# Splitting two inner products of a Strassen-Winograd kernel a third time, in its first four stages

## The chip, the cores and the metric

The kernel runs on one core of a Trainium2 chip. The core has TensorE (PE; PEld is its weight load), VectorE (DVE), ScalarE (ACT), GpSimd (POOL) and SyncE (SP), each with its own instruction queue in order, and 16 DMA engines. On-chip data lies in SBUF; PE writes its products into PSUM, eight banks of 512 fp32 columns by 128 partitions. The metric is the device time of one execution in microseconds (us), the median of several runs.

## The reference

`x` has 16 x 512 = 8192 rows of 512, `router_logits` 8 values for each row, `expert_weights` eight matrices of 512 x 2048. The output is the sum of all experts' products, weighted by the softmax:

```python
probs = np.exp(router_logits - logits_max)
probs = probs / np.sum(probs, axis=-1, keepdims=True)
for e in range(n_experts):
    output += probs[:, :, e:e+1] * np.matmul(x, expert_weights[e])
```

With the weighted copies of `x` side by side this is one product of 8192 x 4096 by 4096 x 2048.

## The kernel before

**Two levels of Strassen-Winograd.** The large product is cut in halves in each of its three dimensions and made from seven products, named P1 to P7 (`product(r, q)`, r from 1 to 7), instead of eight. Rows come in 16 pairs of blocks of 256 (`HQ`), so each P has 16 instances, q from 0 to 15. An instance is again cut in two by two by two and made from seven *inner* products: 128 rows (`HP`) by 1024 contracted values (eight chunks of 128) by 512 columns, that is eight matmuls of 512 columns (`Product.step`). `STEPS` gives their order, 1, 5, 6, 2, 7, 3, 4. In Winograd's form some products are sums of earlier ones: 6, 7 and 4 are added by PE onto the bank that inner product 1 wrote ("x"), 3 onto that of 5 ("q"), 2 onto a copy ("b") of 1. Between these additions ACT or DVE takes the intermediate values out (`Product.post`, `post_alone` for P1).

**Operands.** The left operand of an instance (`Left`) is made by DVE from transposed rows `xT` and broadcast probabilities `pT`: two halves (`make`, tiles `z`, 2048 columns each), their difference `s2` (tile `d`) and `i` (a `z`). The right operand (`Right`) is a set of fp16 weight tiles `w`, some read, some summed by DVE (`inner_sums`). In an early part the instances P1 of q = 0 and 1 are computed in another way (loop over `n` and `e`, lines 308 to 331), in which the weights are read, transposes are made on PE, and ACT finally copies four banks out (line 331).

**Stages.** From then on the work runs in stages of mostly two instances, step by step in turn (`run`): 14 steps of eight matmuls. Stages 0 to 3 hold the P1 instances of q = 2 to 9, two in each; stage 4 pairs a P2 with a P1.

**Order of the work.** Each engine's queue keeps the program's order. DVE's background work (left operands, weight sums) stands in one queue of tasks with costs written into the code. `slack` advances a PE clock by 1.73 us (`SLOT`) for every step and takes tasks off the queue while DVE's clock is behind; `need` takes off everything up to an operand that a step is about to use; `evacuated` books an evacuation on DVE. Loads, stores and weight casts hang on a stage's step number: loads for the stage after next start after step 1 (`start_loads`), stores after 5, transposing DMAs after 7 (`finish_loads`), others through `hooks`, set by `at(stage, slot, ...)`.

**Buffers.** Weight tiles `w` 15 (`wpool`), `z` 8, `d` 3, `x` 10, `h` 12 (`hpool`: halves of results waiting for their store, and small temporaries), PSUM banks 8 (`bank`).

Of the kernel before, what the change touches and what calls it, by code (L numbers as in the profile page):

```python
# [31 lines left out]
def kernel(  # L32
# [7 lines left out]
    nc = tc.nc  # L40
    P = 128
    f16 = mybir.dt.float16
    f32 = mybir.dt.float32
    ADD, SUB, MUL = mybir.AluOpType.add, mybir.AluOpType.subtract, mybir.AluOpType.mult
# [5 lines left out]
    C = H // P  # L50
# [4 lines left out]
    HQ = 256  # L55
# [15 lines left out]
    K8 = 2 * C  # L71
    BLOCKS = ((0, 0), (1, 0), (0, 1), (1, 1))

    def h_tile(shape, dtype):
        return hpool.tile(shape, dtype, name="h", tag="h")

    def half():
        return h_tile([P, NB], f32)
# [16 lines left out]
    def note(i):  # L95
        last[i.ins.engine] = i.ins
        if ordered[0]:
            tc.keep_in_program_order(i)

    def dve(i):  # L100
        last[i.ins.engine] = i.ins
        tc.keep_in_program_order(i)

    act = dve

    def tt(o, a, b, op):
        dve(nc.vector.tensor_tensor(out=o, in0=a, in1=b, op=op))  # L107
# [15 lines left out]
    def bank():  # L123
        return psum.tile([P, NB], f32, name="ps", tag="ps")

    def mm(ps, z, w, start, stop):
        note(nc.tensor.matmul(ps, z, w, start=start, stop=stop, skip_group_check=True))  # L127
# [3 lines left out]
    def new_w():  # L131
        return wpool.tile([P, K8, NB], f16, name="w", tag="w")
# [31 lines left out]
    def inner_sums(b, t7=None):  # L164

        w = {1: b[0, 0], 2: b[1, 0], 3: b[1, 1], 7: t7 or b[0, 1]}

        def step(p, x, y):
            if p not in w:
                w[p] = new_w()  # L170
            tt(w[p], x, y, SUB)
        return w, {5: lambda: step(5, b[0, 1], b[0, 0]), 6: lambda: step(6, b[1, 1], w[5]),
                   4: lambda: step(4, b[1, 0], w[6]), 7: lambda: step(7, b[1, 1], b[0, 1])}

    def softmax(lg, J, pf):
        mx = h_tile([P, J], f32)
        dve(nc.vector.tensor_reduce(out=mx, in_=lg, axis=AX, op=mybir.AluOpType.max))
        tt(lg, lg, mx.unsqueeze(2).to_broadcast([P, J, E]), SUB)
        nc.scalar.activation(out=lg, in_=lg, func=mybir.ActivationFunctionType.Exp)
        sm = h_tile([P, J], f32)  # L180
        dve(nc.vector.tensor_reduce(out=sm, in_=lg, axis=AX, op=ADD))
        dve(nc.vector.reciprocal(out=sm, in_=sm))
        n = pf.shape[1]
        tt(pf, lg.rearrange("p j e -> p e j")[:, 0:n], sm.unsqueeze(1).to_broadcast([P, n, J]), MUL)
        return pf
# [35 lines left out]
    def early_p(t):  # L221
        if t == 0:
            return softmax(lg0[t], 4, cpool.tile([P, HE, 4], f16, name="ph0"))
        pf = softmax(lg0[t], 4, cpool.tile([P, HE, 4], f32, name="pf0"))
        odd = pf.rearrange("p e (q j) -> p e q j", j=2)[:, :, :, 1]
        tt(odd[:, 0:2], odd[:, 0:2], odd[:, 2:4], ADD)
        ph = cpool.tile([P, HE, 4], f16, name="ph1")
        dve(nc.vector.tensor_copy(ph, pf))
        return ph
# [16 lines left out]
    def diag_e(e):  # L246
        return diag(ph0[0][:, e].unsqueeze(2))

    def early_z0(e, d):
        for j in range(4):  # L250
            ps = bank()
            for c in range(C):
                mm(ps[:, ds(c * P, P)], xs0[:, j, ds(c * P, P)], d[:, j], c == 0, c == C - 1)
            evacuate(z0[j][:, e], ps.rearrange("p (c t) -> p c t", c=C), j)
# [5 lines left out]
    def diag_j(j):  # L260
        return diag(ph0[1][:, :, ds(j % 4, 1)])
# [46 lines left out]
    for n in range(2):  # L308
        ps = [bank() for _ in range(4)]
        for e in range(HE):  # L310
            if n == 0 and e < 2:
                early_z0(e + 2, ds_[e + 2])
                if e == 0:
                    ds_.append(diag_e(3))
            if n == 0 and e == 2:
                ph0.append(early_p(1))
                ds_ = [diag_j(j) for j in range(4, 8)]
                softmax_of_all()
                w, sums = inner_sums(b11, new_w())
            for c in range(C):  # L320
                for j in range(4):
                    mm(ps[j], z0[j][:, e, c], b11[e // 2, n][:, e % 2 * C + c, :],
                       e + c == 0, e == HE - 1 and c == C - 1)
            if n == 1:
                for j in ((4, 5), (6, 7), (), ())[e]:
                    early_xp1(j, ds_[j - 4])
                if e == 1:
                    sums[5]()
        for j in range(4):
            o = half()  # L330
            act(nc.scalar.copy(o, ps[j]))
            sp(kept[j // 2][n].rearrange("(p j) m -> j p m", j=2)[j % 2], o)

    ordered[0] = True
    SLOT = 1.73
    STEPS = (1, 5, 6, 2, 7, 3, 4)
    HP = HQ // 2
    LAG = 0.3
    queue = deque()
    clock = {"pe": 0.0, "dve": 0.0}  # L340

    class Task:


        def __init__(self, cost, make):
            self.cost, self.make, self.done = cost, make, False
# [10 lines left out]
    def need(task):  # L357
        if task is not None and not task.done:
            flush(task)
            clock["pe"] = max(clock["pe"], clock["dve"])  # L360

    def later(cost, make, first=False):
        t = Task(cost, make)
        (queue.appendleft if first else queue.append)(t)
        return t

    def slack():
        clock["dve"] = max(clock["dve"], clock["pe"])
        clock["pe"] += SLOT
        while queue and clock["dve"] < clock["pe"] - LAG:  # L370
            queue.popleft().run()

    def evacuated():
        clock["dve"] = max(clock["dve"], clock["pe"]) + 0.69


    x_dram = {}
# [48 lines left out]
    class Left:  # L426
# [6 lines left out]
        def make(self, k):  # L433
            if self.of is not None:
                need(self.of.task[k])
            t = self.t[k] = new_z()
            times(t, k, self.xb, self.pb)
            if self.less is not None:
                u = new_u()
                times(u, k, *self.less)  # L440
                tt(t, t, u, SUB)
            if self.of is not None:
                tt(t, self.of.t[k], t, SUB)
# [19 lines left out]
        def op(self, p):  # L463
            need(self.task[{1: 0, 5: 0, 6: "s2", 2: 1, 4: 1, 3: "i", 7: "i"}[p]])
            if p == 6:
                return self.s2
            t, i = {1: (self.t[0], 0), 5: (self.t[0], 1), 2: (self.t[1], 0), 4: (self.t[1], 1),
                    3: (self.i, 0), 7: (self.i, 1)}[p]
            return t[:, :, ds(i * HP, HP)]

    class Right:

# [100 lines left out]
    stages = []  # L573
    hooks, late = {}, {}
# [11 lines left out]
    lefts, xs, ps_, bases = {}, {}, {}, {}  # L586
# [69 lines left out]
    def start_loads(stage):  # L656
        if stage < len(stages):
            for p in stages[stage]:
                for load in p.loads:
                    load.begin()  # L660
# [13 lines left out]
    def queue_left(left):  # L674
        if not left.task:
            left.queue_make(0)
            left.queue_s2()
            left.queue_make(1)

    def queue_lefts(stage):  # L680
        if stage < len(stages):
            for p in stages[stage]:
                queue_left(p.left)

    def run(stage):
        some = stages[stage]
        for p in some:
            p.left.queue_i()
        n = 0
        for i in range(len(STEPS)):  # L690
            for p in some:
                for make in hooks.get((stage, n), ()):
                    make()
                p.step(p.steps[i])
                slack()
                p.post(p.steps[i])
                n += 1
                if n == 1:
                    queue_lefts(stage + 1)
                if n == late.get(stage, 1):  # L700
                    start_loads(stage + 2)
                if n == 5:
                    store_loads(stage + 1)
                if n == 7:
                    finish_loads(stage + 2)
# [12 lines left out]
    for i in range(0, 10, 2):  # L718
        k = add(product(2, rest[i]), product(2, rest[i + 1]))
# [9 lines left out]
    some = product(6, 15)  # L729
# [4 lines left out]
    some = product(4, 15)  # L734
# [16 lines left out]
    for q in range(16):  # L751
        k = k5 + 1 + q
# [223 lines left out]
    cols = [ds(i * NB // 2, NB // 2) for i in range(2)]  # L976
# [26 lines left out]
            post(p)  # L1003
    finish.step, finish.post = step_at_end, post_at_end

    need_first = [right[1].task[p] for p in (6, 7, 4)]
    for p in (2, 3):
        lefts[1, p].queue_make(0)
    queue.append(need_first[0])
    for p in (2, 3):  # L1010
        lefts[1, p].queue_s2()
    for p in (2, 3):
        lefts[1, p].queue_make(1)
    queue.extend(need_first[1:])
    start_loads(1)
    store_loads(0)
# [1 line left out]
    for k in range(len(stages)):  # L1018
        run(k)
# [28 lines left out]
```

## Time and profile before

| what | value |
|---|---|
| median of 3 runs | 1376.44 us (1376.37 to 1376.78) |
| profiled execution | 1376.57 us, span 1374.8 us |
| TensorE clock granted | 1.00 |
| PE busy / DVE / ACT / POOL | 1368.2 / 1109.0 / 183.1 / 411.9 us |
| matmuls `ps<-w,z` of 512 columns | 5400, mean 379 ns |
| stages 0 to 3, in the span | 40.26 to 136.9 us |

Rows of the profile name a line of the kernel, the engine, the operation, output tile and inputs, shapes, and the count; after the bar stand busy time, the mean duration of one in ns and the idle time of that engine just before, with what ended it. Line 127 is the helper that issues every matmul, line 107 the one that issues every `tensor_tensor` on DVE. A timeline row gives start, duration, engine, line and what ended the wait before it. Matmuls are pipelined: one of 512 columns is listed with 379 ns, but the next starts earlier than that. The time of a profiled execution holds some microseconds outside the span of its instructions.

### The profile page before, as it was taken

What the parts mean: (1) busy time and instruction counts of PE and PEld (TensorE: products, weight loads), DVE (VectorE), ACT (ScalarE), POOL (GpSimd) and SP (SyncE); (2) the same over time, 40 slices, a digit from 0 to 9 for tenths busy, and PEclk for the clock granted to TensorE, in tenths of its full rate; (3) what the DMA queues carried; (4) which work ended last, traced back from release to release, by engine and by line L of the source; (5) the groups of instructions that cost most, each with busy time, mean ns of one, the idle gap of its engine ahead of it and who ended that gap; (6) DMA issues with size and microseconds to landing.
All of it is one profiled execution on the core that took longest, in us unless ns stands there. A gap on an engine that the chain in (4) does not pass through costs nothing.

```text
span 1374.8 us, 17481 instructions
## 1 busy us (share of the span) xinstructions
PE 1368.2 (100%) x6390; PEld 622.4 (45%) x6390; DVE 1109.0 (81%) x1290; ACT 183.1 (13%) x317; POOL 411.9 (30%) x652
## 2 busy tenths in 40 slices
PE   9999999999999999999999999999999999999998
PEld 4444444444444444444444444444444444444444
DVE  5846757679889888888887988889889898988782
ACT  3221111100011111111111100000000000212221
POOL 3222333231223342434332122333333322232322
PEclk9999999999999999999999999999999999999999
DMA  9998999999898998998897997988898979998785
GB/s 181 218 259 215 213 252 261 252 294 379 239 313 254 266 315 250 278 263 238 255 274 263 333 395 214 232 239 209 227 233 227 241 211 312 249 187 179 167 148 101
DMA packets 191271, 338.02 MB, mean 246 GB/s; under 512 B 52944, under 2 KB 86992, under 8 KB 187472
## 3 DMA queue, kind: packets, MB, share of 16 engines
q0 software_dynamic: 88688, 185.12, 56.2%
q1 hardware_dynamic: 98464, 123.34, 30.7%
q10 hardware_dynamic: 4032, 28.44, 5.3%
q8 instruction: 50, 0.82, 0.3%
q14 instruction: 37, 0.30, 0.1%
HBM read 207.65 MB, written 156.43 MB: 265 GB/s over the span
## 4 chain that ended last, share of the span: by engine, by line
PE 98%; DMA 1%; DVE 0%; issue 0%; POOL 0%; ACT 0%; POOLq 0%
PE ps L127 98%; DMA w<-wd 1%; DMA w<-in_x_dram 0%; DVE h L107 0%; DVE z L241 0%; POOL w L121 0%; ACT h L1000 0%; DVE lg L281 0%; POOLq L1032 0%
## 5 line engine op out<-in xcount | busy, mean ns | idle before, releaser
L127 PE MATMUL ps<-w,z 128*128 128x512 f16 x5416 | 1177.2, 379 | 0.9 <-DVE h L107 0.8
L127 PEld LDWEIGHTS <-z 128*128 128x128 f16 x5416 | 529.8, 98 | 638.1 <-issue 1.1
L121 POOL DMA_DIRECT2D out_dram<-h x380 | 248.9, 672 | 753.4 <-ACT h L540 379.7
L107 DVE TENSOR_TENSOR h<-ps,h 128x512 f32<-128x512 f32 x415 | 282.5, 688 | 209.5 <-PE ps L127 194.5
L107 DVE TENSOR_TENSOR z<-xT,pT 128x2048 f16<-128x2048 f16 x220 | 266.9, 1217 | 12.7 <-DMA xT<-xs 10.1
L127 PE MATMUL ps<-w,d 128*128 128x512 f16 x880 | 199.1, 379 | 0.0
L127 PEld LDWEIGHTS <-d 128*128 128x128 f16 x880 | 86.1, 98 | 103.8
L107 DVE TENSOR_TENSOR z<-z,d 128x2048 f16<-128x2048 f16 x110 | 132.1, 1216 | 0.0
L107 DVE TENSOR_TENSOR w<-w 128x1024 f16<-128x1024 f16 (+2 forms) x92 | 100.8, 1102 | 3.2 <-DMA wd<-w 1.4
L527 ACT COPY h<-ps 128x512 f32<-128x512 f32 x90 | 52.8, 587 | 373.9 <-PE ps L127 326.6
L540 ACT COPY h<-ps 128x512 f32<-128x512 f32 x64 | 37.5, 587 | 485.8 <-PE ps L127 458.5
L107 DVE TENSOR_TENSOR z<-z,u 128x2048 f16<-128x2048 f16 x64 | 78.4, 1225 | 2.2
L107 DVE TENSOR_TENSOR d<-z 128x1024 f16<-128x1024 f16 x110 | 75.2, 685 | 5.9 <-PE ps L127 4.0
L107 DVE TENSOR_TENSOR u<-xT,pT 128x2048 f16<-128x2048 f16 x64 | 77.9, 1218 | 0.0
L523 ACT COPY h<-ps 128x512 f32<-128x512 f32 x90 | 52.8, 587 | 173.9 <-PE ps L127 171.1
L121 POOL DMA_DIRECT2D wd<-w x86 | 48.3, 585 | 33.1 <-DVE w L107 24.4
L121 POOL DMA_DIRECT2D w<-in_expert_weights_dram x65 | 48.9, 784 | 27.8 <-DMA wd<-w 18.0
L107 DVE TENSOR_TENSOR ps<-ps,h 128x512 f32<-128x512 f32 (+1 forms) x66 | 45.4, 689 | 13.0 <-PE ps L127 12.9
L121 POOL DMA_DIRECT2D kept<-h x56 | 30.8, 551 | 76.9 <-ACT h L527 46.9
L107 DVE TENSOR_TENSOR h<-h 128x512 f32<-128x512 f32 (+2 forms) x69 | 45.1, 675 | 0.2
L519 ACT COPY ps<-ps 128x512 f32<-128x512 f32 x45 | 25.6, 570 | 114.6 <-PE ps L127 114.6
L107 DVE TENSOR_TENSOR z<-z 128x2048 f16<-128x2048 f16 x32 | 39.2, 1225 | 1.1
(47 smaller groups left out, 98.4 us busy)
## 6 DMA issues: line engine op xcount, KB each, us to landing
out_dram<-h POOLq DMA_DIRECT2D x380, 256.0 KB, 6.2
pT<-p_dram SPq DMA_DIRECT2D x140, 256.0 KB, 6.1
w<-wd ACTq DMA_DIRECT2D x27, 1024.0 KB, 9.6
h<-kept SPq DMA_DIRECT2D x100, 256.0 KB, 5.4
xT<-x SPq DMA_DIRECT2D x87, 256.0 KB, 5.6
wd<-w POOLq DMA_DIRECT2D x72, 256.0 KB, 5.4
w<-in_expert_weights_dram POOLq DMA_DIRECT2D x35, 512.0 KB, 10.0
h<-out_dram SPq DMA_DIRECT2D x68, 256.0 KB, 5.5
```

What stands on the lines that cost most here:

```text
L107: dve(nc.vector.tensor_tensor(out=o, in0=a, in1=b, op=op))
L121: note(nc.gpsimd.dma_start(out=o, in_=i, **how))
L127: note(nc.tensor.matmul(ps, z, w, start=start, stop=stop, skip_group_check=True))
L519: act(nc.scalar.copy(self.banks["b"], x))
L523: act(nc.scalar.copy(o[tn], q if p == 5 else x))
L527: act(nc.scalar.copy(o[TN[p]], b if p == 2 else x))
L540: act(nc.scalar.copy(o[tn], b))
```

## The change

In stages 0 to 3, the inner products 1 and 5 of the two instances are no longer two products each. For each of the two, the pair of instances is taken as one product of 256 rows (128 of each instance) by 1024 by 512, which is cut a third time: rows between the two instances, the contracted values into two groups of four chunks, the columns into two halves of 256. Seven products of four matmuls of 256 columns take the place of two of eight matmuls of 512. Steps of the new level are called r1 to r7 here, in the order of `STEPS`, and inner products 1 and 5 take turns at each.

The new right operands are made once (`third_sums`, four `tensor_tensor` for inner product 1 and four for 5, each set in one further weight tile) in the early part, and `sums[5]` moves one `e` forward. The new left operands of a stage are four sums of 128 x 1024 (`Thirds.make`, one task of cost 2.76 for both inner products, since they lie in the two row halves of the same tiles). Each of the two inner products has a spare bank beside its two result banks: r1, r6, r7, r4 use the left 256 columns of it, r5 and r3 the right, and ACT or DVE moves the values on. DVE's queue is ordered anew, and the hooks of a stage's first four steps run at the small steps 0, 4, 7 and 11.

```diff
+    def third_sums(w):
+        t = new_w().rearrange("p (s c) (h n) -> p s c h n", s=2, h=2)
+        t = {5: t[:, 0, :, 0], 6: t[:, 0, :, 1], 7: t[:, 1, :, 0], 4: t[:, 1, :, 1]}
+        b = w.rearrange("p (k c) (h n) -> p k c h n", k=2, h=2)
+        tt(t[5], b[:, 0, :, 1], b[:, 0, :, 0], SUB)
+        tt(t[6], b[:, 1, :, 1], t[5], SUB)
+        tt(t[7], b[:, 1, :, 1], b[:, 0, :, 1], SUB)
+        tt(t[4], b[:, 1, :, 0], t[6], SUB)
+        return {**t, 1: b[:, 0, :, 0], 2: b[:, 1, :, 0], 3: b[:, 1, :, 1]}
...
                 w, sums = inner_sums(b11, new_w())
+                third = {1: third_sums(w[1])}
...
-                if e == 1:
+                if e == 0:
                     sums[5]()
+                elif e == 1:
+                    third[5] = third_sums(w[5])
...
-    def slack():
+    def slack(slot=SLOT):
         clock["dve"] = max(clock["dve"], clock["pe"])
-        clock["pe"] += SLOT
+        clock["pe"] += slot
...
+    class Thirds:
...
+        def make(self):
+            e0, e1 = ds(0, C), ds(C, C)
+            a, b = self.a.t[0], self.b.t[0]
+            for p, x, y, op in ((5, b[:, e0], b[:, e1], ADD), (6, None, a[:, e0], SUB),
+                                (3, a[:, e1], None, SUB), (7, a[:, e0], b[:, e0], SUB)):
+                o = self.s[p] = h_tile([P, C, HQ], f16)
+                x = self.s[5] if x is None else x
+                y = self.s[6] if y is None else y
+                tt(o, x, y, op)
+
+        def queue(self):
+            self.a.queue_make(0)
+            self.b.queue_make(0)
+            self.task = later(2.76, self.make)
+            for left in (self.a, self.b):
+                left.queue_s2()
+            for left in (self.a, self.b):
+                left.queue_make(1)
+
+        def op(self, p, part):
+            need(self.task)
+            a, b = self.a.t[0], self.b.t[0]
+            z = {1: a[:, 0:C], 2: a[:, C:K8], 4: b[:, C:K8]}.get(p)
+            return (self.s[p] if z is None else z)[:, :, ds(part * HP, HP)]
...
+    def by_thirds(stage):
+        some = stages[stage]
+        left = thirds[stage]
+        cols = [ds(i * HQ, HQ) for i in range(2)]
+        goals, spare, kept_ = {}, {}, {}
+        for i, (p, b) in enumerate(((1, "x"), (5, "q"))):
+            for product in some:
+                product.banks[b] = bank()
+            goals[p] = [product.banks[b] for product in some]
+            spare[p], kept_[p] = bank(), half()
+        slot = 0
+        for n, (r, p) in enumerate((r, p) for r in STEPS for p in (1, 5)):
+            if n in (0, 4, 7, 11):
+                for make in hooks.get((stage, slot), ()):
+                    make()
+                slot += 1
+                if slot == 2:
+                    queue_lefts(stage + 1)
+                    start_loads(stage + 2)
+            (g, h), t, keep = goals[p], spare[p], kept_[p]
+            x, q = t[:, cols[0]], t[:, cols[1]]
+            o = {1: x, 6: x, 7: x, 4: x, 5: q, 3: q, 2: g[:, cols[0]]}[r]
+            z, w = left.op(r, p // 5), third[p][r]
+            for c in range(C):
+                mm(o, z[:, c, :], w[:, c, :], r == 1 and c == 0, c == C - 1)
+            slack(0.4375)
+            if r == 1:
+                act(nc.scalar.copy(g[:, cols[0]], x))
+            elif r == 5:
+                act(nc.scalar.copy(keep[:, cols[1]], q))
+            elif r == 6:
+                act(nc.scalar.copy(keep[:, cols[0]], x))
+            elif r == 7:
+                evacuated(0.42)
+                tt(h[:, cols[1]], x, keep[:, cols[1]], ADD)
+            elif r == 3:
+                evacuated(0.42)
+                tt(g[:, cols[1]], q, keep[:, cols[0]], ADD)
+                if p == 1:
+                    some[0].post(1)
+            elif r == 4:
+                act(nc.scalar.copy(h[:, cols[0]], x))
+        some[1].post(1)
+        for product in some:
+            product.post(5)
+        return 4
...
     def queue_lefts(stage):
-        if stage < len(stages):
+        if stage in thirds:
+            if thirds[stage].task is None:
+                thirds[stage].queue()
+        elif stage < len(stages):
...
-        n = 0
-        for i in range(len(STEPS)):
+        n = by_thirds(stage) if stage in thirds else 0
+        for i in range(n // 2, len(STEPS)):
...
+    for stage in range(4):
+        thirds[stage] = Thirds(*(p.left for p in stages[stage]))
     need_first = [right[1].task[p] for p in (6, 7, 4)]
-    for p in (2, 3):
-        lefts[1, p].queue_make(0)
-    queue.append(need_first[0])
-    for p in (2, 3):
-        lefts[1, p].queue_s2()
-    for p in (2, 3):
-        lefts[1, p].queue_make(1)
+    thirds[0].queue()
+    queue.insert(3, need_first[0])
     queue.extend(need_first[1:])
```

More of the change, by code (lines that the diff above doesn't have):

```diff
@@ L365, in later, with evacuated @@
         return t
-    def slack():
+    def slack(slot=SLOT):
         clock["dve"] = max(clock["dve"], clock["pe"])
-        clock["pe"] += SLOT
+        clock["pe"] += slot
         while queue and clock["dve"] < clock["pe"] - LAG:
             queue.popleft().run()
-    def evacuated():
-        clock["dve"] = max(clock["dve"], clock["pe"]) + 0.69
+    def evacuated(cost=0.69):
+        clock["dve"] = max(clock["dve"], clock["pe"]) + cost
     x_dram = {}
@@ L469, in op, with __init__ @@
             return t[:, :, ds(i * HP, HP)]
+    class Thirds:
+        def __init__(self, a, b):
+            self.a, self.b, self.s, self.task = a, b, {}, None
+        def make(self):
[20 more added lines that the diff above has]
+            return (self.s[p] if z is None else z)[:, :, ds(part * HP, HP)]
     class Right:
@@ L678, in queue_left @@
             left.queue_make(1)
+    thirds = {}
+    def by_thirds(stage):
[44 more added lines that the diff above has]
+        return 4
     def queue_lefts(stage):
-        if stage < len(stages):
+        if stage in thirds:
+            if thirds[stage].task is None:
+                thirds[stage].queue()
+        elif stage < len(stages):
             for p in stages[stage]:
```

## The prediction, made before the result was known

> **What bounds the kernel now.** I read the page first: engine shares, the chain that ended last, the costliest groups.
>
> ```profile
> span 1374.8 us, 17481 instructions
> PE 1368.2 (100%) x6390; PEld 622.4 (45%) x6390; DVE 1109.0 (81%) x1290; ACT 183.1 (13%) x317; POOL 411.9 (30%) x652
> PE 98%; DMA 1%; DVE 0%; issue 0%; POOL 0%; ACT 0%; POOLq 0%
> L127 PE MATMUL ps<-w,z 128*128 128x512 f16 x5416 | 1177.2, 379 | 0.9 <-DVE h L107 0.8
> ```
>
> TensorE is the path: its 5416 products waited 0.9 us in all. A matmul taken away is a gain, a wait put in is a loss, one for one. Next the four stages that the change rewrites: busy time in windows cut at their starts (first four steps of stage 0, rest of it, stages 1, 2, 3; the first column after the window is its length, then PE, PEld, DVE, ACT, POOL), and the chain in order of time.
>
> ```profile
> 40.26:47.16 6.90, 6.90 (x33) 3.13 (x32) 6.90 (x7) 3.33 (x7) 0.71 (x1) 1.00 0.85 251
> 47.16:64.42 17.26, 17.26 (x81) 7.84 (x80) 13.12 (x14) 3.52 (x6) 6.13 (x10) 1.00 1.20 225
> 64.42:88.59 24.17, 24.17 (x113) 10.94 (x112) 12.57 (x14) 5.83 (x10) 7.32 (x12) 1.00 1.19 247
> 9.08 251.06 PE ps L127 x1198
> ```
>
> PE has no gap here, the clock is full (1.00), DVE and ACT have room by share, but in the first 6.9 us of stage 0 DVE has none. Then the rows that price the new work: TensorE's forms, and from the timeline of the last stage the only place where PE waits for the reader of a bank and where 256 columns are evacuated.
>
> ```profile
> L127 PE MATMUL ps<-w,z 128*128 128x256 f16 x16 | 1.9, 272 | 0.0
> ...
> 1362.93 0.38 PE L127 MATMUL ps<-w,d 128*128 128x512 f16 x1
> 1363.35 0.69 DVE L107 TENSOR_TENSOR h<-ps,h 128x512 f32<-128x512 f32 x1 [1.03 <-PE ps L127]
> 1364.09 0.38 PE L127 MATMUL ps<-w,z 128*128 128x512 f16 x1 [0.78 <-DVE h L107]
> ...
> 1370.34 0.42 DVE L997 COPY h<-ps 128x256 f32<-128x256 f32 x1 [0.18 <-PE ps L127]
> 1371.21 0.37 ACT L1000 COPY h<-ps 128x256 f32<-128x256 f32 x1 [12.42 <-PE ps L127]
> ```
>
> Last, ACT at the start of stage 0 and DVE at the start of stage 2 (timeline):
>
> ```profile
> 39.81 2.05 ACT L331 COPY h<-ps 128x512 f32<-128x512 f32 x4 [5.62 <-PE ps L127]
> 42.24 0.57 ACT L519 COPY ps<-ps 128x512 f32<-128x512 f32 x1 [0.38 <-PE ps L127]
> ...
> 91.21 1.23 DVE L107 TENSOR_TENSOR z<-xT,pT 128x2048 f16<-128x2048 f16 x1 [2.83 <-DMA xT<-xs]
> 92.47 0.69 DVE L107 TENSOR_TENSOR d<-z 128x1024 f16<-128x1024 f16 x1
> 93.08 1.22 DVE L107 TENSOR_TENSOR z<-xT,pT 128x2048 f16<-128x2048 f16 x1
> 94.90 1.23 DVE L107 TENSOR_TENSOR z<-xT,pT 128x2048 f16<-128x2048 f16 x1 [0.60 <-DMA xT<-xs]
> ```
>
> ACT is four copies behind when stage 0 begins (40.26), which costs nothing today. DVE waits for transposed x in stage 2, hidden too. Call inner product 1's seven small products A, inner product 5's B; r1A is step r1 of A.
>
> **Matmuls: removed against added.** Start to start a 512-column matmul takes 6.90/32 = 0.216 us, a 256-column one (1.9 - 0.272)/15 = 0.109. Four steps of 8 go, 4 x 8 x 0.216 = 6.90; 56 small ones come, 56 x 0.109 = 6.12. That is -0.79 per stage, **-3.15** in four. Weight loads rise from 32 to 56 at 98 ns, still under 109; in the last stage 16 such pairs ran at that spacing.
>
> **The spare bank, the wait that is added.** In each chain r1, r6, r7, r4 write the left half of one bank and r5, r3 the right half, and between them ACT or DVE reads the half just finished. Before, no bank is written in one half while the other half is read, so the trace doesn't price it. Lower bound: nothing, the halves being apart. Upper: the whole wait of the last-stage rows. I take the upper, as it is nearest to those rows, the only ones where a bank is written right after it is read, and there PE stood until the read was over; where the old kernel evacuates halves (L997, L1000) each has a bank of its own. The wait: last matmul of four starts at 3 x 0.109, ends 0.272 later; the reader starts 0.04 after the end (1362.93 + 0.38 to 1363.35), reads 0.37 (ACT) or 0.43 (DVE), PE starts 0.05 later (1363.35 + 0.69 to 1364.09). So 1.06 or 1.12 us from one step of a chain to the next, where two chains of four fill only 0.87. Added: r5 to r6 0.19, r7 to r3 0.24, r3 to r4 0.24. B follows A by 0.44 and adds nothing. At r1 to r5 ACT is also busy with the last copy of the stage before: it starts 0.2 into the stage, the next follows 0.48 later (2.05 for four), reads until 1.04, so r5A starts at 1.09, +0.22. Together 0.90: the steps take 7.01 for 6.90, **+0.10 each in stages 1 to 3, +0.31**.
>
> The Trainium skill's page "PSUM — Partial Sum Buffer", section "PSUM bank collisions raise a hardware error", says that two engines must not be in one bank at once, even in different columns, and that waits are to be set by bank, not by address. By it the sum is the upper one, +1.7; by halves that are independent it would be -2.4 (below). No row here decides, and the rule speaks against the change.
>
> **ACT in stage 0.** Its four copies hold it until 39.81 + 4 x 0.48 = 41.73; then it reads r1A until 42.09, and r5A starts at 42.14, 1.88 into the stage and not 0.87: +1.01. With 0.19 + 0.24 + 0.24 the steps take 7.80, **+0.90**, ending at 48.06 and not 47.16.
>
> **DVE in stage 0.** Going through the two clocks of the planner with the listed costs gives this order: sum 6, both s2, four evacuations, both second left halves, sums 7 and 4, the first i, the second i, evacuation of step 7. Back to back DVE needs 1.14 for a left half (2.35 for two), 2.20 for a sum. Evacuation of r3B starts about 47.13; then 0.35, 2 x 1.14, 2 x 2.20 and 1.22 for the first i: it is ready at 55.4. Step 7 needs it at 48.06 + 4 x 1.726 = 54.95. **+0.47**. In the old order it had 4 us to spare (ready 48.78 + 1.22 = 50.0, needed 40.26 + 8 x 1.726 = 54.1). Next late after it: the first evacuation of step 7, without effect (bank wanted 5 us later).
>
> **What is hidden.** The sums of w1 (four tt of 1024 columns, row 685 ns, 0.60 apart: 2.4) fall into a DVE gap of 3.08 us before 28.57; those of w5 (2.4) take the place of sum 5, which goes one expert forward, where DVE was idle. The left halves are then ready at 37.8 and 38.9 for 40.26, the first left sum at 39.5 for 41.1; if that cover of 1.6 us is gone, stage 0 starts its r5 late by the rest. In stages 1 to 3 the four left sums (2.4), two extra halves to `h` and eight 256-column copies on ACT lie beside PE; the 1.22 us task planned just before the evacuation of r7A is normally done, since DVE runs ahead. Loads start at the fifth small step (about 1.8 us) where they started at 1.73; SP and POOL queues move by less than the stage does; the weight casts tied to slots 2 and 3 come up to 0.4 us earlier. Two more weight tiles make at most 15 alive, the pool's size; six more `h` tiles come to about 11 of 12. No wait there shows in the old rows; from nothing to one landing of a store (8.2 us, the median of kept<-h here) in place of a free buffer: I take nothing, and keep it for the upper end.
>
> **Sum.** 0.31 + 0.90 + 0.47 = +1.68 against the profiled execution: 1376.57 (span 1374.8, 1.8 around it), 0.13 above the median of 1376.44. So 1376.44 + 1.7 = **1378.1**, own range 1376.7 to 1379.6.
>
> **Rivals.**
> *The halves don't wait for each other.* For it: nothing seen either way. Then the stage takes 6.12; r6A still waits for ACT's late r1 copy (0.13), and step 7 of stage 0, now due at 53.4 with its i ready at 54.0, loses 0.62: -3.15 + 0.75 = -2.4, **1374.0**. Even without these two it is 1373.3.
> *Slower: DVE stands before a bank reader.* In stage 2 the planned order puts the first left half of stage 3 ahead of the evacuation of r7A. That product started at 91.21, 2.6 after the stage's start, waiting for x; the evacuation is due at 4.53 and the product takes 1.14, so it decides from a landing 3.4 after the start: 0.8 to spare. Past that each us late is a us lost, since r3A waits for that read. At the second block's offset (94.90, 6.3) it costs 2.9: **1381.0**. For it: DMA share over 1 in these windows, and a 5.95 us wait for x one stage earlier. Against: PE gets there 1.4 us later, and the transposes are chained to one another, not to PE.
> *Same sums, no stall in stage 0* (ACT's copies done in time, i early): 1376.7, in the likeliest's range.
>
> **How the numbers follow.** Likeliest 0.58. Halves independent 0.12. DVE or a buffer late 0.30, 1379.3 to 1384. A measurement tells about 0.2% from no change, 2.75 us: 1373.7 to 1379.2. Faster 0.05 (part of the second case), slower 0.34 (nearly all of the third, a little of the first), same 0.61. Range 1373.9 to 1382.0: it takes in the second case and two thirds of the third.
>
> **What would show it.** Right: small matmuls 0.109 apart within a step, the first four steps' worth 7.0 us in stages 1 to 3 and 7.8 in stage 0; PE's waits before r5 and r6 named ACT, before r3 and r4 DVE; the first r5 of stage 0 about 1 us late behind the fourth L331 copy; step 7 of stage 0 waiting for an i on DVE; nothing changed after stage 3. Wrong: no gap between r1 and r5 (second case); PE waiting for DVE behind a z product in stage 2, or for a store of `h` (third); small matmuls over 0.11 apart.

## The result, and the profile after

The changed kernel takes 1381.12 us in the median of nine runs (1379.01 to 1388.66), the kernel before 1376.78 in nine (1376.25 to 1378.32): ratio 1.0039, 95% interval 1.0027 to 1.0051. It is slower by 4.3 us, and its times scatter over 9.6 us where those of before scatter over 2.1. The profiled execution is one of its fastest, 1379.63 us, 3.06 above the profiled one of before.

The page after, and from the grouped lines TensorE's forms (busy time, mean ns | idle before, and what ended it):

```profile
span 1377.9 us, 17744 instructions
PE 1367.9 (99%) x6486; PEld 631.6 (46%) x6486; DVE 1130.3 (82%) x1330; ACT 192.9 (14%) x349; POOL 411.8 (30%) x652
L127 PE MATMUL ps<-w,z 128*128 128x512 f16 x5384 | 1161.5, 377 | 2.5 <-DVE h L107 1.5
...
L127 PE MATMUL ps<-w,h 128*128 128x256 f16 x128 | 16.7, 271 | 1.9 <-ACT ps L755 0.9 <-DVE ps L107 0.3
L127 PE MATMUL ps<-w,z 128*128 128x256 f16 x112 | 14.3, 272 | 0.6 <-DVE ps L107 0.6
```

(The first row of forms merges 5272 matmuls of 512 columns with the 112 of the last row.) PE's busy time hardly fell and its idle time rose, with ACT and DVE named, both readers of PSUM. The small steps of stages 0 to 3 in windows from the first r1 to the first matmul of step 6 (after the window: length, then PE, PEld, DVE, ACT, POOL):

```profile
39.71:47.70 7.99, 6.76 (x57) 5.43 (x56) 7.10 (x11) 4.45 (x12) 0.00 (x0) 1.00 0.91 263
65.44:72.90 7.46, 6.91 (x57) 5.44 (x56) 4.72 (x8) 3.48 (x9) 2.78 (x5) 1.00 1.13 274
90.17:97.32 7.15, 6.75 (x57) 5.43 (x56) 2.95 (x5) 3.52 (x9) 0.54 (x1) 1.00 1.12 197
114.59:121.74 7.15, 6.75 (x57) 5.43 (x56) 3.11 (x6) 3.52 (x9) 2.67 (x4) 1.00 1.06 258
```

Each of these took 6.90 us before and would take 6.12 without a gap. So even in the good execution no stage gains: +1.09, +0.56, +0.25, +0.25. The timeline of stage 0 shows where:

```profile
39.27 2.05 ACT L345 COPY h<-ps 128x512 f32<-128x512 f32 x4 [5.62 <-PE ps L127]
...
41.18 0.69 ACT L755 COPY ps<-ps 128x256 f32<-128x256 f32 x2
41.65 2.09 PE L127 MATMUL ps<-w,h 128*128 128x256 f16 x16 [0.90 <-ACT ps L755]
...
45.16 0.87 DVE L107 TENSOR_TENSOR ps<-ps,h 128x256 f32<-128x256 f32 x2 [0.53 <-PE ps L127]
45.64 1.03 PE L127 MATMUL ps<-w,h 128*128 128x256 f16 x8 [0.16 <-DVE ps L107]
...
46.34 0.87 DVE L107 TENSOR_TENSOR ps<-ps,h 128x256 f32<-128x256 f32 x2 [0.32 <-PE ps L127]
...
46.83 1.03 PE L127 MATMUL ps<-w,z 128*128 128x256 f16 x8 [0.16 <-DVE ps L107]
```

r5 of the first chain (41.65) waits until ACT, behind its four old copies, has read r1 (L755 from 41.18); r3 (45.64) and r4 (46.83) wait for DVE. The idle figures (0.90, 0.16) are counted from the modelled end of the last matmul; start to start, beyond the 0.109 us of one matmul, the waits are 1.06, 0.32, 0.32, and 0.19 before r6. In stages 1 to 3 they are 0.24, 0.19, and twice 0.31 to 0.32, and once, in stage 1, 0.29 more behind a copy of r1 in the second chain that ACT starts 0.4 us late; the profile names nothing but the copy before it. Step 7 of stage 0 waits 0.46 for its i.

The difference of the two profiled spans, 3.1 us, is then: 2.15 in the small steps, 0.46 before step 7, 0.67 more at one wait near 800 us (0.25 before; the same matmul, for which the profile names a weight transfer before and DVE after), 0.35 at the very end, less 0.54 in the first 40 us, whose loads vary in both kernels. Most other runs are slower still, by something that this execution doesn't show.

### The profile page after: what moved, and what is told of

Same layout as the page of the kernel before. It is cut to its first block, busy times and chain, and to the rows that moved or that the text cites. A ratio compares the mean times of both kernels' runs of the same rounds, so it can differ in the third digit from the quotient of the medians.

```text
span 1377.9 us, 17744 instructions
## 1 busy us (share of the span) xinstructions
PE 1367.9 (99%) x6486; PEld 631.6 (46%) x6486; DVE 1130.3 (82%) x1330; ACT 192.9 (14%) x349; POOL 411.8 (30%) x652
## 4 chain that ended last, share of the span: by engine, by line
PE 95%; DVE 0%; ACT 0%; issue 0%; DVEq 0%; ACTq 0%
PE ps L127 95%; DVE ps L107 0%; ACT h L572 0%; DVE h L107 0%; ACT ps L755 0%; DVE z L107 0%; ACT h L759 0%; ACT h L1098 0%; DVEq L107 0%; ACTq L755 0%
## 5 line engine op out<-in xcount | busy, mean ns | idle before, releaser
L127 PE MATMUL ps<-w,z 128*128 128x512 f16 x5384 | 1161.5, 377 | 2.5 <-DVE h L107 1.5
L107 DVE TENSOR_TENSOR w<-w 128x1024 f16<-128x1024 f16 (+2 forms) x100 | 106.0, 1068 | 3.5 <-DMA wd<-w 1.7
L107 DVE TENSOR_TENSOR ps<-ps,h 128x512 f32<-128x512 f32 (+1 forms) x82 | 52.2, 638 | 20.7 <-PE ps L127 16.8
```

## The experiments

**Two more traces of the changed kernel.**

> The changed kernel again, unaltered, for a second trace. Its nine times run from 1379.0 to 1388.7 us, the profiled one is at the low end (1379.6). If the waits in stages 0 to 3 vary, the sum of TensorE's extra intervals there, 5.8 us in the first trace, differs by as much as the time does. If it is a late transfer elsewhere, that sum stays at 5.8 and the wait at about 800 us (0.93) or a new one grows. If it is TensorE's clock, intervals between matmuls are twice as long for some microseconds and no wait is named.

> As the look before it: a third draw of the same kernel. The three explanations predict the same as there.

1381.39 and 1380.47 us. The regular waits are the same to 0.01 us. The second has no other in these stages; its 0.84 us over the trace above lies in its first 40 us (1.21 longer) less 0.37 at the waits behind 800 us. The first has one more: before r3 in stage 2 PE loses 1.92 us where 0.31 was usual. DVE there:

```profile
89.79 1.22 DVE L107 TENSOR_TENSOR z<-z,d 128x2048 f16<-128x2048 f16 x1
96.33 1.23 DVE L107 TENSOR_TENSOR z<-xT,pT 128x2048 f16<-128x2048 f16 x1 [5.33 <-DMA xT<-xs]
97.47 0.76 DVE L107 TENSOR_TENSOR ps<-ps,h 128x256 f32<-128x256 f32 x2
```

The product of transposed rows, an operand of stage 3, waits 5.33 us for x, and the evacuation that PE needs stands behind it. It starts 5.09 us after the stage (91.24); in the trace shown above and in the other of these two 2.86 and 2.88. The clock stays full. Against the trace above its first 40 us are also 1.07 longer, by late loads, and the wait of 0.93 near 800 us is absent. So it is the first of the three explanations, a wait in these stages, that the extra 1.6 us bears out.

**A long execution of the changed kernel**, timed beside the two remedies below.

> The changed kernel unaltered, timed beside the two that follow. Times from 1379 up to 1385 or more, median about 1381, as in its first nine; the low end is where x for stage 3 lands in time.

1384.03 us median of six (1379.2 to 1388.42), before 1377.2: ratio 1.0051 (1.0033 to 1.0069). The profiled execution took 1388.42. Its timeline in stage 2:

```profile
100.77 1.23 DVE L107 TENSOR_TENSOR z<-xT,pT 128x2048 f16<-128x2048 f16 x1 [8.75 <-DMA xT<-xs]
101.55 0.47 SPq L118 DMA_DIRECT2D x<-xT  x1
101.91 0.76 DVE L107 TENSOR_TENSOR ps<-ps,h 128x256 f32<-128x256 f32 x2
102.39 1.01 PE L127 MATMUL ps<-w,h 128*128 128x256 f16 x4 [5.54 <-DVE ps L107]
```

and its windows around that place, the granted clock after POOL:

```profile
97.00:101.40 4.40, 0.00 (x0) 0.00 (x0) 0.63 (x1) 0.00 (x0) 0.00 (x0) 1.00 1.14 208
101.40:108.40 7.00, 6.01 (x23) 3.27 (x23) 5.64 (x10) 2.77 (x6) 2.24 (x3) 0.51 1.06 230
108.40:115.40 7.00, 7.00 (x34) 3.19 (x33) 3.78 (x5) 2.34 (x4) 0.92 (x2) 1.00 1.18 190
```

x came 9.2 us after the stage's start and PE stood idle for 5.54 us, from 96.85 to 102.39. The granted clock was 0.5 from 101.55 to 108.38, and 22 intervals between matmuls in that time took 5.9 us for the 3.0 that they take at full clock (16 of 0.109 and six of 0.216). From step 6 of stage 1 to step 6 of stage 3 it took 8.3 us longer than the first trace; 5.39 of that is the wait (5.70 less the usual 0.31), 2.9 the clock. The Trainium skill's page "TensorE: Matmul & The Clock Gate", section "Why this matters for your kernels", says that a gap of more than some 3 us puts the clock back to half. This trace agrees with 5.54 us of idling, and so does that of the 1381.39 us execution with 1.76 us idle there and no loss of clock.

**The left operands late.**

```diff
                 if slot == 2:
-                    queue_lefts(stage + 1)
                     start_loads(stage + 2)
...
         for product in some:
             product.post(5)
+        queue_lefts(stage + 1)
         return 4
```

> One line moved: the left operands of the next stage are queued after the small steps and not among them, so that no product of transposed rows stands on DVE before an evacuation that TensorE waits for. Nothing is left out. If that product causes the spread (the second look lost 1.62 us there beyond the usual 0.31), the upper part of the times goes: 1379 to 1380.5, median about 1379.7, and no wait before r3 over 0.4 us. If the spread comes from elsewhere, for instance the loads in the first 10 us or the weight fetch at 800 us, the times stay as wide as those of the changed kernel.

1379.59 us, 1378.37 to 1380.59 in eleven, against 1384.03 and up to 1388.42 for the changed kernel beside it; ratio to before 1.0017 (1.0008 to 1.0026). The upper part is gone, and no wait before r3 exceeds 0.32. With the product out of the way the evacuations come at once:

```profile
95.83 0.87 DVE L107 TENSOR_TENSOR ps<-ps,h 128x256 f32<-128x256 f32 x2 [4.84 <-ACT h L758]
97.02 0.87 DVE L107 TENSOR_TENSOR ps<-ps,h 128x256 f32<-128x256 f32 x2 [0.32 <-PE ps L127]
97.80 2.35 DVE L107 TENSOR_TENSOR z<-xT,pT 128x2048 f16<-128x2048 f16 x2
```

So one place in DVE's order made the scatter and half to two thirds of the loss: 4.4 of 6.8 us between the medians measured together here, 2.0 of 4.3 by the first nine runs, each kernel taken against the kernel before beside it. The 2.4 us that remain are about what the regular waits add up to less the gain in matmuls (2.15 + 0.46 = 2.6).

**Is x late in the kernel before, too?** Three more traces of it.

> The kernel before, unaltered, for a second trace of when x for stage 3 is there. In its first trace the product of transposed rows starts 2.6 us after stage 2. If the landing scatters whatever the kernel, and the old order only hides it, some of these three looks have it 3.4 us or more after the start of stage 2, with the time still near 1377. If the change makes x late, all three stay near 2.6.

> A third trace of the kernel before, for the landing of x for stage 3; the two explanations expect the same as in the first of these looks.

> A fourth trace of the kernel before, for the landing of x for stage 3; the two explanations expect the same as in the first of these looks.

1377.19, 1376.45, 1377.19 us. The product starts 1.26, 3.39 and 0.07 us after stage 2 (2.60 in the first trace), and in the changed kernel 2.86, 5.09, 2.88 and 9.16. So neither explanation holds as it was put: none of the looks reaches 3.4, and none stays near 2.6. It scatters in both kernels. It is later in the changed one, though four traces against four leave room for chance.

Two things lie ahead of the product: the cast of x on POOL, then a transposing DMA. The cast does go out later, and the runs tell by what. In stage 0 its first one starts 3.6 us after the stage's start in all four traces of the kernel before and 10.7 to 11.0 in all four of the changed kernel; in stage 1 it is 1.7, 1.8, 5.2 and 1.6 before and 4.7, 6.3, 4.1 and 5.1 after. The run with late left operands has 10.8 and 4.7, of the experiments below the one with the third split in stage 0 alone 10.8 and 4.8, and the one that leaves stage 0 as it was 3.8 and 1.8. So it is the new order of stage 0 that delays the casts, and not the split of the later stages; for stage 1 this rests on one trace of each.

But the late cast doesn't explain the two long waits. The first transposing DMA for stage 3 is issued 12.2 to 14.1 us after the start of stage 1 before and 11.0 to 14.8 after, and the execution of 1381.39 us has the earliest, 11.0. What is longest in the two late executions is the transfer. From issue to landing, for the transposing DMAs around there, first in the first trace of the kernel before, then in the execution of 1381.39 us:

```profile
DMA to landing us min/median/max: 6.8/8.9/13.0
DMA to landing us min/median/max: 2.8/11.2/17.2
```

The longest is 17.2 and 17.8 us in the two late executions, 12.3 and 13.2 in the other two of the changed kernel, 10.6 to 13.0 in the four of the kernel before. What makes it long, and whether the late casts have a part in it, wasn't tried and stays open.

**A bank for each half.**

```diff
-            spare[p], kept_[p] = bank(), half()
+            spare[p], kept_[p] = [bank(), bank()], half()
...
-            x, q = t[:, cols[0]], t[:, cols[1]]
+            x, q = t[0][:, cols[0]], t[1][:, cols[1]]
...
-                mm(o, z[:, c, :], w[:, c, :], r == 1 and c == 0, c == C - 1)
+                mm(o, z[:, c, :], w[:, c, :], r in (1, 5) and c == 0, c == C - 1)
```

(The spare banks are also taken from the pool ahead of the others.)

> The two halves of each spare bank become two banks: r1, r6, r7, r4 write one, r5 and r3 another. Nothing is left out. If the waits between steps that share a bank are the loss, all of them before r5, r6, r3 and r4 go (about 1.05 us a stage, more in stage 0), the first four steps' worth takes 6.1 to 6.3 us, and the kernel comes to 1375 to 1376 us, at or under the kernel before. If halves of a bank don't wait and the gaps are the readers' lateness, the gaps stay and so does the time, 1379 to 1381. If the loss beyond the profiled one has another source, the spread of times stays 5 us or more wide.

The instructions are the same, but, contrary to the expectation, part of the sums is not formed: a group's first matmul un-marks a whole bank of which only half is then written, and where such a bank is used next, additions to the other half replace it. The Trainium skill's page "PSUM — Partial Sum Buffer", section "The four PSUM rules", describes this; no row here shows it by itself. The time is that of the same work. It took 1378.25 us (1375.25 to 1380.1 in eleven), before 1376.88: ratio 1.0012 (1.0003 to 1.0021). Windows of the small steps:

```profile
40.16:46.74 6.58, 6.44 (x58) 5.48 (x57) 6.55 (x11) 4.00 (x12) 0.00 (x0) 1.00 0.82 243
64.64:70.80 6.16, 6.16 (x57) 5.49 (x56) 4.46 (x8) 3.33 (x9) 1.17 (x3) 1.00 1.16 289
88.07:95.95 7.88, 6.43 (x57) 5.46 (x56) 2.88 (x6) 3.32 (x9) 0.97 (x2) 1.00 1.06 219
113.22:119.38 6.16, 6.16 (x58) 5.49 (x57) 2.85 (x6) 3.33 (x9) 2.67 (x4) 1.00 1.05 269
```

Stages 1 and 3 fall from 7.46 and 7.15 to 6.16. The wait was for the other half of the same bank. It stands in the program: r3's first matmul waits on a semaphore of DVE in the changed kernel and on none here. No run lets PE write one half while the other is read, so what the chip would do without the wait isn't shown. Stage 0's 1.06 goes too; 0.47 remain there, and step 7 of stage 0 waits 0.63 for its i where it waited 0.46, since the steps before it are shorter. Stage 2 holds 1.7 us of a late product, which this edit doesn't touch. So the expected 1375 to 1376 was missed, and the times still spread over 4.9 us.

**Stage 0 alone.**

```diff
-    for stage in range(4):
+    for stage in range(1):
         thirds[stage] = Thirds(*(p.left for p in stages[stage]))
```

> The third split in stage 0 alone; stages 1 to 3 run as in the kernel before. Nothing is left out. By the sum of the first trace stage 0 costs its waits 1.89 and the wait for i 0.46 less 0.79 of matmuls, +1.6 us, and the rest nothing: 1378.3. By the rival, that the loss is the same in every stage, a quarter of +4.3: 1377.9; by the rival that stages 1 to 3 hold the spread, times within 2 us of each other here.

1378.91 us (1378.05 to 1380.28), before 1376.88: ratio 1.0017 (1.0008 to 1.0026). The trace has stage 0's waits as before (1.06, 0.19, 0.32, 0.32, and 0.46 before step 7) and none in stages 1 to 3. They predict 1.55 over the kernel before, 2.03 was measured; a quarter of the loss would be 1.1. The interval, 1.1 to 3.6 us, doesn't decide between the two; the waits in the trace do. Runs lie within 2.3 us: the scatter doesn't show with stage 0 alone.

**Both remedies, in stages 1 to 3.** DVE sets the used halves of four spare banks to zero in the stage before (`zero`, a task of four memsets, put at the head of its queue at slot 10), and no group on these banks then un-marks one, so that every sum is formed; stage 0 is as in the kernel before.

```diff
+    def zero(stage):
+        spare = {p: [bank(), bank()] for p in (1, 5)}
+        def make():
+            for i in range(2):
+                for p in (1, 5):
+                    dve(nc.vector.memset(spare[p][i][:, 0:HQ], 0.0))
+        zeroed[stage] = spare, later(1.2, make, True)
...
-                mm(o, z[:, c, :], w[:, c, :], r == 1 and c == 0, c == C - 1)
+                mm(o, z[:, c, :], w[:, c, :], False, c == C - 1)
...
+        queue_lefts(stage + 1)
         return 4
...
-    for stage in range(4):
+    for stage in range(1, 4):
         thirds[stage] = Thirds(*(p.left for p in stages[stage]))
+        at(stage - 1, 10, lambda stage=stage: zero(stage))
```

> The third split in stages 1 to 3 only, with both remedies: left operands late as in the run before, and two banks for each chain, whose used halves DVE sets to zero in the stage before. Nothing is left out. If same-bank waits and the late product are all that ate the gain, each of the three stages keeps most of 0.79 us: about -2.0 us against the kernel before, 1374.5 to 1375.5, with a spread like that kernel's. If the third split costs something more that no wait shows, it stays at 1376 or above.

1374.83 us (1373.86 to 1375.63 in eleven), before 1377.2: ratio 0.9983 (0.9974 to 0.9991). That is 2.4 us faster than the kernel before, three times 0.79, and 9.2 faster than the changed kernel timed beside it. Its small steps, in the same windows:

```profile
65.28:71.44 6.16, 6.16 (x57) 5.47 (x56) 4.46 (x8) 3.33 (x9) 1.82 (x4) 1.00 1.25 226
88.70:94.87 6.17, 6.17 (x58) 5.49 (x57) 2.34 (x6) 3.33 (x9) 0.54 (x1) 1.00 1.29 181
112.13:118.28 6.15, 6.15 (x58) 5.48 (x57) 1.94 (x5) 3.33 (x9) 2.68 (x4) 1.00 1.00 240
```

Length and PE's busy time are equal: no wait is left, and in these stages the third split costs nothing that a wait doesn't show. Stage 0 with both remedies wasn't tried. The largest extra interval in the stages is 0.05 us.

## Why the prediction was right or wrong

The forecast was no change that can be told, 1378.1; it came out slower, 1381.12, inside the range and in the third case, which had 0.30.

- **Matmuls, -3.15.** Right: 0.109 us apart in every step, and the best version's steps take 6.15 to 6.17 for a predicted 6.12.
- **The spare bank.** Right in kind: PE does wait for the read of the other half, as the upper bound had it. The case of independent halves falls with the bank-for-each-half run, whose stage 0 also shows that case's own terms: 0.19 before r6A for 0.13, and 0.63 before step 7 for 0.62. Sizes: r5 to r6 0.19 as predicted, r1 to r5 0.24 for 0.22, the two DVE waits 0.31 to 0.32 for 0.24, since DVE starts 0.11 us after the last matmul's end (45.156 after 45.048) and not the 0.04 of the old row: a semaphore instruction of DVE, at 45.090, stands between. With stage 1's late r1 copy, stages 1 to 3 lost 1.06 us and not 0.31.
- **ACT in stage 0.** Right: 1.06 for 1.01. With DVE's later starts the steps took 7.99 for 7.80.
- **DVE in stage 0.** Right: 0.46 for 0.47 (the terms listed there add up to 0.43). The i and the step that needs it both came 0.2 us later than reckoned.
- **Sum of these.** 2.6 us in the traces, 2.4 between the medians of the late-operand run and the kernel before, for 1.68. Too small by a third, mostly through those DVE starts.
- **What is hidden.** This is the step that failed: "the 1.22 us task planned just before the evacuation of r7A is normally done, since DVE runs ahead", taken at nothing. It held in two of four traces. In the other two x was there 5.09 and 9.16 us after the start of stage 2, and PE lost 1.62 and 5.39 us. The third case had named the mechanism, the place and the price: deciding point 3.4 us after the stage's start, then a us for a us, which gives 1.7 and 5.8. What was wrong was its chance. The 0.8 us to spare came from one trace; four traces of that kernel go from 0.07 to 3.39, so the margin was as good as used up in one of them. That its 1381.0 all but meets the median is luck: it stood for a landing 6.3 us late on top of 1.68, and the median holds 2.4 us of regular waits and about 2 that go with late left operands. In one execution a loss of clock after the long wait added half of the wait's price; it was not foreseen.
- **The queues.** "SP and POOL queues move by less than the stage does" failed too: the first cast of x in stage 0 moved by 7 us, stage 0 grew by 1.6. What this costs isn't shown. The argument against the third case, that the transposes are chained to one another and not to PE, is not settled: they were issued about as early as before, and two of them took longer to land.
- **Nothing after stage 3.** Right. The wait near 800 us goes from nothing to 0.93 us in four traces of the changed kernel and from nothing to 1.23 in four of the kernel before: it scatters in both. At the very end, behind the last matmul, all four traces of the changed kernel are 0.35 us longer than the four of the kernel before; why isn't known.

## What to carry to other kernels

Count a bank of PSUM as one thing between TensorE and its readers: two groups that use halves of a bank in turn run one after the other with the whole turn-around between them (here 1.06 to 1.2 us) where the program waits by bank, so give each its own bank or put enough other steps between. When a step gets shorter, look at what stands ahead of its evacuation in the queue of that engine: work that waits for a transfer belongs behind it. And a margin read from one trace of a scattering transfer is not a margin; take several traces before calling the cover safe.

## What the runs showed of the hardware that was not expected

- In an idle time of 5.54 us on TensorE the granted clock fell to 0.5, 4.7 us after its start, and stayed there for 6.8 us, which cost another 2.9 us; idle times of 1.8 us and less cost nothing more.
- DVE's start after TensorE's last matmul was 0.04 us in the old last stage, where the evacuation itself waits on the semaphore, and 0.11 in the small steps, where a semaphore instruction of DVE stands ahead of it (45.090, then 45.156).
- The start of the same product, which waits for x's transposing transfers, scattered by 3.3 us in four traces of the kernel before and by 6.3 us in four of the changed one; the longest of these transfers took 10.6 to 13.0 us in the former and 12.3 to 17.8 in the latter.
